# Attention scores of a two-layer trunk in three rounded terms, with the scores of heads 0 to 3 behind the second q projection

## The chip, the cores and the metric

The kernel runs on one core of one Trainium2 chip. The metric is the time of the whole program on the device in microseconds. Before the change three runs gave a median of 249.99 us (249.98 to 250.0).

## What is computed

Two layers of a decoder trunk over 256 positions of width 1024. Each layer normalises x, projects it with one matrix of 3584 columns, and feeds three branches: eight heads of a mixture of dilated causal attention, a linear recurrence of width 256, and four heads of stick-breaking attention. The branches are gated and projected back. For this change these parts of the reference matter:

```
qa = apply_partial_rope(a_q.reshape(b, s, N_HEADS_DIL, HEAD_DIM), cos, sin)   # 8 heads of 64
ka = apply_partial_rope(a_k.reshape(b, s, N_HEADS_DIL, HEAD_DIM), cos, sin)
...
s = jnp.einsum('bhqd,bhqjd->bhqj', q_blk, k_g)            # dilated: the union of three patterns
...
z = jnp.einsum('bhqd,bhkd->bhqk', q_blk, kf) * scale      # stick-breaking, 4 heads, no rope
...
y = jnp.concatenate([y_a, y_b, y_c], axis=-1)
return x + jnp.einsum('bse,ed->bsd', y, w_out)
```

All inputs and outputs are float32. The kernel computes every score of a head as a product of q and k over 64 dimensions: query tile 0 (queries 0 to 127) against 128 keys, query tile 1 against 256 keys, the causal and pattern masks being added afterwards.

## The kernel before

Activations are held transposed, so that a projection of 256 columns gives q or k of four heads as two blocks of 128 partitions, two heads of 64 dimensions in each. The weights come from memory in chunks of 1 MB (`load_chunk`, L101): each is loaded in two halves, and each quarter is rounded on ScalarE (L109, tile `whi`) and its rest formed on VectorE (L110, `wlo` = weight minus `whi`). Activations are split alike (`xh`, `xl`). A projection is the sum of three rounded matmul products, high by high, high by rest and rest by high (`mm3`, L211; in layer 1 `proj_b` joins two of them, L329 and L332, and adds the parts on VectorE, L337). The chunks go through four buffers and are asked for up to two ahead (`ask`, `weights`).

The order on TensorE is the program's order, written by hand; on the other engines a scheduler arranges the instructions of the same program, and each engine then runs its list in order. `proj_b` takes an argument `mid`: work that is put between the two halves (blocks of 128 columns) of a projection. In a layer the projections of this stretch come in this order: q and k of the stick-breaking heads (`qc`, `kc`), q and k of dilated heads 0 to 3 (`CH_AQ[0]`, `CH_AK[0]`), the recurrence's input (`CH_BX`, inside `conv`), q and k of heads 4 to 7 (`CH_AQ[1]`, `CH_AK[1]`), then the gates CG, BG and AG.

Scores are plain float32 matmuls (L443 for the stick-breaking heads in `sb_scores`, L497 for the dilated heads in `dil_scores`). A call makes four heads; the two heads of a pair use different halves of TensorE's rows and stand next to each other in the order. Each head's scores fill one PSUM bank (128 x 384 used) of the pool `at`, which has four banks under the tag "s"; the transposes of weights and probabilities (`turned`, L463) and the gate matmuls use the same four in turn. Projections use three banks of the pool `pp`.

Behind the stick-breaking scores ScalarE makes two sigmoids a head (L449, L450, shown at L83) and VectorE two scans and a product (L454, L456). Behind the dilated scores VectorE subtracts the mask and takes the row minimum (L504), ScalarE exponentiates, and VectorE divides (L515, L517). q and k of the dilated heads are rotated on VectorE (`rotate`, L481 to L484). The convolution is VectorE work as well (L544, L546), and GpSimd sends its result to memory positions in the other half (L549). GpSimd does little else: small constants at the start of the program (L274 to L290), two single-column operations per norm, and clearing one column pair per head (L452).

Of the kernel before, what the change touches and what calls it, by code (L numbers as in the profile page):

```python
# [9 lines left out]
F32 = mybir.dt.float32  # L10
# [5 lines left out]
P = 128  # L16
# [32 lines left out]
def trunk_kernel(ctx: ExitStack, tc: tile.TileContext, x, first_x, first, wpack, prm_d, gatew, gains, consts, rope, out):  # L49
# [247 lines left out]
    for l in range(L):  # L297
# [5 lines left out]
        def y_half(h):  # L303
            ys[h] = [sb.tile([P, 4, S], F32R, name=n, tag=f"{n}{h}") for n in ("yh", "yl")]

        y_half(0)

        def proj_a(ps, w, t, kb, nk, cw, first, last):
            v = [a.rearrange("p (k c) -> p k c", c=cw) for a in w]
            ts_ = slice(t * P, t * P + P)  # L310
# [3 lines left out]
        def proj_b(c, mid=None, to=None, sc=1.0):  # L314
            pair = c in PAIRED[l]
            hi, lo = [a.rearrange("p (k c) -> p k c", c=256) for a in weights(l, c, AHEAD - 1 if mid else AHEAD)]
            if pair:
                flat = None if to is not None else scr(512)
                to = v2(flat) if to is None else to
            else:  # L320
                flat = bank(pp, "pp")
            for b in range(2):
                cs = slice(b * P, b * P + P)
                if pair:
                    ps = bank(pp, "pp")
                    seq = [(0, k) for k in range(NK - 1)] + [(1, k) for k in range(NK)] + [(0, NK - 1)]
                    for i, (is_lo, k) in enumerate(seq):
                        if is_lo:
                            pe.matmul(ps[:, 0:S], lo[:, k, cs], xh[:, k, :], start=False, stop=False,  # L329
                                      skip_group_check=True)  # L330
                        else:
                            pe.matmul(ps, hi[:, k, cs], xx[:, k].rearrange("p h t -> p (h t)"), start=i == 0,  # L332
                                      stop=i == len(seq) - 1, skip_group_check=True)
                    low = wk.tile([P, S], F32, name="low", tag="low", bufs=2)
                    act.activation(low, ps[:, S:2 * S], AF.Copy, scale=sc)  # L335
                    if sc == 1.0:
                        dve.tensor_add(to[:, b, :], ps[:, 0:S], low)  # L337
                    else:
                        dve.scalar_tensor_tensor(to[:, b, :], ps[:, 0:S], sc, low, ALU.mult, ALU.add)
                else:  # L340
                    mm3(flat[:, b * 256:(b + 1) * 256], [lambda k, a=a: a[:, k, cs] for a in (hi, lo)],
                        [lambda k, a=a: a[:, k, :] for a in (xh, xl)], range(NK), True, True)
                if b == 0 and mid:
                    mid()
                    ask(l, c)
            return flat

        def proj_to(dst, c, mid=None, sc=1.0):
            if l > 0 and c in PAIRED[l]:
                proj_b(c, mid, dst, sc)  # L350
            else:
                scaled(dst, proj_b(c, mid), sc)
# [65 lines left out]
        def head(h):  # L418
            return slice((h % 2) * HD, (h % 2) * HD + HD), h // 2, slice(h * HD, (h + 1) * HD)
# [13 lines left out]
        zs, sw = {}, {}  # L433
        halves = ((0, slice(0, 128)), (1, slice(128, 384)))

        def sb_scores():
            for p in (0, 2):
                for h in (p, p + 1):
                    zs[h] = bank(at, "s")
                for t, cs in halves:  # L440
                    for h in (p, p + 1):
                        hr, hb, _ = head(h)
                        pe.matmul(zs[h][:, cs], qc[hr, hb, t * P:(t + 1) * P], kc[hr, hb, 0:(t + 1) * P],  # L443
                                  start=t == 0, stop=True, skip_group_check=True)
            table(SIGM, [split[l, CH_AK[0]]])
            for h in range(NHC):
                z = zs[h][:, 0:384]
                bt, om = scr(384), scr(384)
                tab(om, z, AF.Sigmoid, scale=-1.0)  # L449
                tab(bt, z, AF.Sigmoid)  # L450
                w = sw[h] = wk.tile([P, 384], F32, name="sw", tag="sw", bufs=4)
                gps.memset(w[:, 127::256], 0.0)  # L452
                for lo, n in ((0, 127), (128, 255)):
                    dve.tensor_tensor_scan(w[:, lo:lo + n][:, ::-1], om[:, lo + 1:lo + 1 + n][:, ::-1],  # L454
                                           diag[:, 255 - n:255][:, ::-1], 0.0, ALU.mult, ALU.add)
                dve.tensor_mul(w, bt, w)  # L456
# [19 lines left out]
        def rotate(ps, tiles, h0, tag):  # L476
            dst = tiles[h0] = sb.tile([P, 2, S], F32, name=tag, tag=tag)
            rt_ = rp0 if l == 0 else rp
            cc, ss = [rt_[:, i:i + 1, :].broadcast_to([P, 2, S]) for i in range(2)]
            sw = scr(512)  # L480
            dve.stream_shuffle(sw, ps, SHUF)  # L481
            dve.tensor_mul(dst, v2(ps), cc)
            dve.tensor_mul(v2(sw), v2(sw), ss)
            dve.tensor_add(dst, dst, v2(sw))  # L484
# [3 lines left out]

        def dil_scores(h0):
            sps = {}  # L490
            for p in (h0, h0 + 2):
                for h in (p, p + 1):
                    sps[h] = bank(at, "s")
                for t, cs in halves:
                    for h in (p, p + 1):
                        hr, hb, _ = head(h - h0)
                        pe.matmul(sps[h][:, cs], qT[h0][hr, hb, t * P:(t + 1) * P], kT[h0][hr, hb, 0:(t + 1) * P],  # L497
                                  start=True, stop=True)
            shifted = {}
            for h in range(h0, h0 + 4):  # L500
                xs = scr(384)
                mn = wk.tile([P, 2], F32, name="mn", tag="mn", bufs=4)
                for t, cs in halves:
                    dve.tensor_tensor_reduce(xs[:, cs], sps[h][:, cs], nmask[:, cs], -0.125, 3e38,  # L504
                                             ALU.add, ALU.min, mn[:, t:t + 1])
                shifted[h] = xs, mn
            return shifted
# [26 lines left out]
        it = sb.tile([P, 2, S], F32, name="it", tag="it")  # L534
        th = sb.tile([P, 2, S], F32, name="th", tag="th")
        bg = sb.tile([P, 2, S], F32, name="bg", tag="bg")
        ag = sb.tile([P, 4, S], F32, name="ag", tag="ag")
        cg = sb.tile([P, 2, S], F32, name="cg", tag="cg")

        def conv(mid):  # L540
            dve.memset(bxp[:, :, 0:3], 0.0)
            proj_to(bxp[:, :, 3:259], CH_BX, mid)
            for b in range(2):
                dve.tensor_scalar(xc[:, b, :], bxp[:, b, 3:259], prm[:, b, 3:4], prm[:, b, 4:5], ALU.mult, ALU.add)  # L544
                for j in (2, 1, 0):
                    dve.scalar_tensor_tensor(xc[:, b, :], bxp[:, b, j:j + 256], prm[:, b, j:j + 1], xc[:, b, :],  # L546
                                             ALU.mult, ALU.add)
            for j in range(2):
                gps.dma_start(out=xs[j * HD:(j + 1) * HD], in_=xc[(1 - j) * HD:(2 - j) * HD])  # L549
# [38 lines left out]
        if l == 0:  # L588
            ck_ps = proj_b(CH_CK, rows_of_rstd)
            scaled(qc, cq_ps, 0.125)  # L590
            scaled(kc, ck_ps)
        else:
            proj_to(kc, CH_CK)
        if l == 0:
            for i in range(2):
                dve.tensor_mul(rp0[:, i, :], rp[:, i, :], rb)
        rotate(proj_b(CH_AQ[0], sb_scores), qT, 0, "q0")
        rotate(proj_b(CH_AK[0]), kT, 0, "k0")
        sw_t, sw_heads = turned_tile()
        conv(lambda: turned(sw, 0, (0,), sw_t))  # L600
        turned(sw, 0, (1, 2), sw_t)
        y_c = {}

        def second():
            table(LN_EXP)
            dil_softmax(dil_scores(0))

        rotate(proj_b(CH_AQ[1], second), qT, 4, "q1")
        rotate(proj_b(CH_AK[1]), kT, 4, "k1")
        table(SIGM)  # L610
        cg_ps = proj_b(CH_CG)
        pts = dil_transposes(0)
        silu(cg, cg_ps)


        def third():
            lru_gates()
# [7 lines left out]
        lru_scan()  # L625
        emit_y(rt, bg, 0, 2)
        dil_softmax(y_c["s"])
        ps = proj_b(CH_AG)
        table(SIGM)
        silu(ag[:, 0:2, :], ps)  # L630
# [145 lines left out]
```

## Time and profile before

| what | value |
|---|---|
| median of three runs | 249.99 us |
| the profiled execution: device time | 248.82 us |
| the profiled execution: span | 246.7 us |
| granted TensorE clock, mean | 0.996 |
| TensorE matmuls busy | 239.0 us (97% of the span) |
| VectorE busy | 196.5 us (80%) |
| ScalarE busy | 167.2 us (68%) |
| GpSimd busy | 12.1 us (5%) |

The profile is one execution. Its device time is 1.2 us below the median of the runs, and 2.1 us above its own span. In its rows PE is TensorE, DVE VectorE, ACT ScalarE, POOL GpSimd and SP the queue that issues most transfers. A row of the chain that ended last has start, length and what ran; a row of a timeline has start, length, engine, line, operation, tiles, shape and count, and in brackets the idle time before it with what ended it. A float32 matmul stands in the rows as two instructions, so a call of eight score matmuls is x16.

### The profile page before, as it was taken

Reading aid. Unit: us, or ns where it says so; the run is one execution under the profiler, and the core shown is the slowest. Engines: PE = TensorE matmul, PEld = TensorE weight load, DVE = VectorE, ACT = ScalarE, POOL = GpSimd, SP = SyncE. Lnnn points to the kernel's source line nnn. Section 1 sums busy time; section 2 is a strip of 40 time slices with the busy share of each in tenths; the row PEclk is TensorE's granted clock in tenths of the full one; section 3 lists DMA queues with packets and bytes.
Section 4 is the critical chain, followed back from the end, with each engine's and each line's share of the span. In section 5 each row is a group of like instructions: output and inputs, shape, how many; then the busy total and the mean of one; then the engine's idle time right before and its main releaser. Section 6 shows DMA issues by size and latency. Waiting matters only on the chain.

```text
span 246.7 us, 4531 instructions
## 1 busy us (share of the span) xinstructions
PE 239.0 (97%) x1657; PEld 212.1 (86%) x1657; DVE 196.5 (80%) x442; ACT 167.2 (68%) x360; POOL 12.1 (5%) x45
## 2 busy tenths in 40 slices
PE   8999999999999999999999999999999999999990
PEld 4889999999998899878889988889889889987870
DVE  3885699999999799985792766999999987985253
ACT  3778989735947499964662885865498649992142
POOL 0037000001000000000100000000010000000000
PEclk9999999999999999999999999999999999999998
DMA  6989889268447741277157486605553672000022
GB/s 201 404 292 403 342 288 333 96 215 268 134 157 255 258 117 56 85 240 284 74 189 232 142 268 243 200 7 165 161 157 119 197 262 98 0 0 3 0 85 85
DMA packets 13173, 43.89 MB, mean 178 GB/s; under 512 B 1632, under 2 KB 2144, under 8 KB 13152
## 3 DMA queue, kind: packets, MB, share of 16 engines
q1 hardware_dynamic: 12384, 42.30, 51.1%
q10 hardware_dynamic: 576, 0.79, 0.9%
q0 software_dynamic: 192, 0.52, 0.7%
q8 instruction: 13, 0.21, 0.4%
q14 instruction: 8, 0.07, 0.1%
HBM read 42.03 MB, written 1.05 MB: 175 GB/s over the span
## 4 chain that ended last, share of the span: by engine, by line
PE 94%; DMA 2%; DVE 1%; ACT 1%; SPq 0%; issue 0%; ACTq 0%
PE pp L211 51%; PE pp L332 11%; PE s L211 9%; PE pp L329 5%; PE s L169 4%; PE s L463 3%; PE s L497 2%; PE y L427 2%; DMA st<-first 2%; PE pp L169 2%; PE s L443 1%; PE pp L427 1%; PE s L557 1%; PE s L259 1%; DVE xres L668 0%; ACT scr L242 0%
## 5 line engine op out<-in xcount | busy, mean ns | idle before, releaser
L110 DVE TENSOR_TENSOR wlo<-st,whi 128x512 fp32r<-128x512 f32 x132 | 84.1, 683 | 12.8 <-ACT whi L109 12.5
L109 ACT ACTIVATE whi<-st 128x512 fp32r<-128x512 f32 x132 | 73.9, 629 | 28.0 <-PE pp L211 11.8
L211 PE MATMUL pp<-xx,whi 128*128 128x256 f32 x480 | 63.3, 285 | 0.0
L211 PEld LDWEIGHTS pp<-xx,whi 128*128 128x128 f32 x480 | 59.7, 191 | 1.4 <-issue 1.3
L211 PE MATMUL pp<-xx,wlo 128*128 128x256 f32 x240 | 33.7, 283 | 0.0
L211 PEld LDWEIGHTS pp<-xx,wlo 128*128 128x128 f32 x240 | 30.9, 192 | 0.0
L332 PE MATMUL pp<-xx,whi 128*128 128x512 f32 x112 | 29.3, 396 | 0.0
L332 PEld LDWEIGHTS pp<-xx,whi 128*128 128x128 f32 x112 | 20.1, 189 | 4.1 <-ACT scr L83 0.3
L77 ACT ACT_TABLE_LOAD x13 | 16.7, 1283 | 1.9 <-PEq L769 1.7
L83 ACT ACTIVATE pr<-scr,mn 128x128 f32<-128x128 f32 (+1 forms) x32 | 14.1, 442 | 5.2 <-DVE mn L504 5.2
L329 PEld LDWEIGHTS pp<-xx,wlo 128*128 128x128 f32 x112 | 15.3, 190 | 1.1
L329 PE MATMUL pp<-xx,wlo 128*128 128x256 f32 x112 | 15.6, 282 | 0.0
L211 PE MATMUL pp<-whi,yh 128*128 128x512 f32 x48 | 14.5, 403 | 0.0
L211 PE MATMUL pp<-wlo,yh 128*128 128x512 f32 x48 | 14.0, 393 | 0.0
L211 PE MATMUL pp<-whi,yl 128*128 128x512 f32 x48 | 14.0, 393 | 0.0
L335 ACT ACTIVATE low<-pp 128x256 f32<-128x256 f32 x14 | 5.3, 382 | 9.1 <-PE pp L332 6.8
L211 PEld LDWEIGHTS pp<-wlo,yh 128*128 128x128 f32 x48 | 9.0, 188 | 2.1
L211 PEld LDWEIGHTS pp<-whi,yl 128*128 128x128 f32 x48 | 9.0, 188 | 2.0
L211 PEld LDWEIGHTS pp<-whi,yh 128*128 128x128 f32 x48 | 8.6, 188 | 2.0 <-issue 0.3
L169 PE MATMUL s<-whi,xx 128*128 128x512 f32 (+1 forms) x36 | 10.2, 404 | 0.1
L415 ACT ACTIVATE yh<-scr 128x512 fp32r<-128x512 f32 x8 | 5.0, 631 | 7.7 <-DVE scr L413 7.6
L504 DVE CUSTOM_DVE_ANT_0 scr<-s,con 128x128 f32<-128x128 f32 (+1 forms) x32 | 9.2, 351 | 0.0
(165 smaller groups left out, 355.2 us busy)
## 6 DMA issues: line engine op xcount, KB each, us to landing
st<-w_pack SPq DMA_DIRECT2D x66, 512.0 KB, 5.4
st<-first SPq DMA_DIRECT2D x7, 512.0 KB, 6.2
xres<-x_in SPq DMA_DIRECT2D x2, 512.0 KB, 8.1
gw_t<-gate_w SPq DMA_DIRECT2D x2, 256.0 KB, 6.9
gn<-gains SPq DMA_DIRECT2D x1, 512.0 KB, 6.7
xs<-xc POOLq DMA_DIRECT2D x4, 128.0 KB, 3.7
gf<-gains SPq DMA_DIRECT2D x1, 512.0 KB, 6.8
out<-scr SPq DMA_DIRECT2D x2, 256.0 KB, 2.1
```

The source lines that it names most:

```text
L77: load = act.preload_act_table_set(name)
L83: i = dep(act.activation(*a, **k), loaded["load"])
L109: split[l, c] = act.activation(hi[:, ws], st[:, ss], AF.Copy)
L110: dve.tensor_sub(lo[:, ws], st[:, ss], hi[:, ws].bitcast(F32))
L169: pe.matmul(ps[t][:, c0 - base:c1 - base], a[:, k, t * P:(t + 1) * P], b[:, c0:c1], start=k == 0 and i == 0 and c0 == base, stop=k == NK - ...
L211: pe.matmul(ps, a(k), b(k), start=first and i == 0, stop=last and i == len(seq) - 1)
L329: pe.matmul(ps[:, 0:S], lo[:, k, cs], xh[:, k, :], start=False, stop=False, skip_group_check=True)
L332: pe.matmul(ps, hi[:, k, cs], xx[:, k].rearrange("p h t -> p (h t)"), start=i == 0, stop=i == len(seq) - 1, skip_group_check=True)
L335: act.activation(low, ps[:, S:2 * S], AF.Copy, scale=sc)
L427: pe.matmul(y[hr, p * 128 + o:p * 128 + 256], vt[:, s0, hs], wts[i][s0], start=s0 == 0, stop=s0 == 1)
L463: pe.transpose(tp[:, i * P:(i + 1) * P], tiles[h0 + h][:, j * P:(j + 1) * P], ident)
L504: dve.tensor_tensor_reduce(xs[:, cs], sps[h][:, cs], nmask[:, cs], -0.125, 3e38, ALU.add, ALU.min, mn[:, t:t + 1])
```

## The change

The plain float32 score matmuls go. A new function `split_keys` rounds q and k of four heads (GpSimd casts q; k is copied by ScalarE for the stick-breaking heads and heads 0 to 3, and cast by GpSimd for heads 4 to 7), and GpSimd forms both rests. `scores` then sums three rounded products per head and query tile: q by k, rest of q by k, q by rest of k. The results are the same scores in the same PSUM banks.

The order changes in four places of each layer. The stick-breaking scores move from the middle of the first q projection into the middle of the first k projection. The scores of heads 0 to 3 and their softmax move from the middle of the second q projection behind it. The transposes of the stick-breaking weights, which stood in the middle of the recurrence's projection and behind it, now stand together behind the second k projection. Without work in the middle, a projection asks for its second chunk ahead at its start. To hold the split tiles, the buffers `yh0`, `yl0`, `ag`, `q0` and `k0` are used before their old owners need them; these are now created later.

```
+        def split_keys(h0, q, k, tags):
+            parts = []
+            for full, tag in ((q, tags[1:]), (k, tags[0])):
+                if full is q and len(tag) == 2:
+                    hi, lo = [sb.tile([P, 2, S], F32R, name="qk3", tag=t) for t in tag]
+                else:
+                    both = sb.tile([P, 2, 2, S], F32R, name="qk3", tag=tag if full is k else tag[0])
+                    hi, lo = both[:, 0], both[:, 1]
+                if full is k and h0 != 4:
+                    act.activation(hi, full, AF.Copy)
+                else:
+                    gps.tensor_copy(hi, full)
+                gps.tensor_sub(lo, full, hi.bitcast(F32))
+                parts.append((hi, lo))
+            (qh, ql), (kh, kl) = parts
+            exact[h0] = (qh, kh), (ql, kh), (qh, kl)
+
+        def scores(ps, h0, p):
+            for t, cs in halves:
+                for n, (a, b) in enumerate(exact[h0]):
+                    for h in (p, p + 1):
+                        hr, hb, _ = head(h)
+                        pe.matmul(ps[h][:, cs], a[hr, hb, t * P:(t + 1) * P], b[hr, hb, 0:(t + 1) * P],
+                                  start=n == 0, stop=n == 2, skip_group_check=True)
...
-                for t, cs in halves:
-                    for h in (p, p + 1):
-                        hr, hb, _ = head(h)
-                        pe.matmul(zs[h][:, cs], qc[hr, hb, t * P:(t + 1) * P], kc[hr, hb, 0:(t + 1) * P],
-                                  start=t == 0, stop=True, skip_group_check=True)
+                scores(zs, "sb", p)
...
+        split_keys("sb", qc, kc, ("yh0", "yl0"))
...
-        rotate(proj_b(CH_AQ[0], sb_scores), qT, 0, "q0")
-        rotate(proj_b(CH_AK[0]), kT, 0, "k0")
-        sw_t, sw_heads = turned_tile()
-        conv(lambda: turned(sw, 0, (0,), sw_t))
-        turned(sw, 0, (1, 2), sw_t)
+        rotate(proj_b(CH_AQ[0]), qT, 0, "q0")
+        rotate(proj_b(CH_AK[0], sb_scores), kT, 0, "k0")
+        split_keys(0, qT[0], kT[0], ("yh0", "yl0"))
+        conv(None)
...
-        rotate(proj_b(CH_AQ[1], second), qT, 4, "q1")
+        q1_ps = proj_b(CH_AQ[1])
+        second()
+        rotate(q1_ps, qT, 4, "q1")
+        sw_t, sw_heads = turned_tile()
         rotate(proj_b(CH_AK[1]), kT, 4, "k1")
+        turned(sw, 0, range(3), sw_t)
+        split_keys(4, qT[4], kT[4], ("ag", "q0", "k0"))
         table(SIGM)
         cg_ps = proj_b(CH_CG)
```

What this does to the lists of the engines shows at three places of layer 0. On TensorE, around the scores of heads 0 to 3, before (each pair of L211 rows is one half of a projection; q_640 and k_709 are q and k of heads 0 to 3, sw the stick-breaking weights):

```order
L463 MATMUL s<-con,sw 128x128 x8
L211 MATMUL pp<-xx,whi 128x256 x16
L211 MATMUL pp<-xx,wlo 128x256 x8
L497 MATMUL s<-k_709,q_640 128x128 x2
L497 MATMUL s<-k_709,q_640 128x256 x2
L497 MATMUL s<-k_709,q_640 128x128 x2
L497 MATMUL s<-k_709,q_640 128x256 x2
L211 MATMUL pp<-xx,whi 128x256 x16
L211 MATMUL pp<-xx,wlo 128x256 x8
```

and now (qk_734 is the split q, qk_737 the split k; the line numbers are those of the changed kernel):

```order
L211 MATMUL pp<-xx,whi 128x256 x16
L211 MATMUL pp<-xx,wlo 128x256 x8
L458 MATMUL s<-qk_737,qk_734 128x128 x6
L458 MATMUL s<-qk_737,qk_734 128x256 x6
L458 MATMUL s<-qk_737,qk_734 128x128 x6
L458 MATMUL s<-qk_737,qk_734 128x256 x6
L211 MATMUL pp<-xx,whi 128x256 x16
L211 MATMUL pp<-xx,wlo 128x256 x8
L211 MATMUL pp<-xx,whi 128x256 x16
L211 MATMUL pp<-xx,wlo 128x256 x8
L484 MATMUL s<-con,sw 128x128 x12
```

The scores stand behind both halves of the second q projection instead of between them, and the twelve transposes of the stick-breaking weights, of which eight stood two rows ahead, follow both halves of the second k projection.

On VectorE, from the end of the rotation of k of heads 0 to 3 to the first reduction of their scores, before (L484 ends the rotation, L392 empties the recurrence's projection, L544 and L546 are the convolution, L504 the reduction):

```order
L484 TENSOR_TENSOR k_709<-k_709,scr 128x512
L110 TENSOR_TENSOR wlo<-st,whi 128x512 x6
L392 SCALAR_TENSOR_TENSOR bxp<-pp,rb 128x2x256
L110 TENSOR_TENSOR wlo<-st,whi 128x512
L544 TENSOR_SCALAR xc<-bxp,prm_t 128x256 x2
L546 SCALAR_TENSOR_TENSOR xc<-bxp,prm_t,xc 128x256 x6
L504 ISA scr,mn<-s,con 128x128
```

and now:

```order
L505 TENSOR_TENSOR k_728<-k_728,scr 128x512
L110 TENSOR_TENSOR wlo<-st,whi 128x512 x3
L390 SCALAR_TENSOR_TENSOR bxp<-pp,rb 128x2x256
L110 TENSOR_TENSOR wlo<-st,whi 128x512
L560 TENSOR_SCALAR xc<-bxp,prm_t 128x256 x2
L562 SCALAR_TENSOR_TENSOR xc<-bxp,prm_t,xc 128x256 x6
L110 TENSOR_TENSOR wlo<-st,whi 128x512 x6
L521 ISA scr,mn<-s,con 128x128
```

Six rests of weights stand between the convolution and the reductions, where there were none; three fewer stand ahead of it.

On GpSimd, between the last of the small constants and its transfers of the convolution's result in layer 0 (qk_523 and qk_526 are the split q and k of the stick-breaking heads), the difference is:

```order
 L290 TENSOR_SCALAR nc_290<-c_289 128x4
-L452 MEMSET sw 128x2 x4
-L549 DMA xs<-xc 64x512 x2
+L447 CAST qk_523<-qc 128x512
+L448 TENSOR_TENSOR qk_523<-qc,qk_523 128x512
+L448 TENSOR_TENSOR qk_526<-kc,qk_526 128x512
+L447 CAST qk_734<-q_594 128x512
+L448 TENSOR_TENSOR qk_734<-q_594,qk_734 128x512
+L448 TENSOR_TENSOR qk_737<-k_728,qk_737 128x512
+L565 DMA xs<-xc 64x512 x2
```

Six operations of 128x512 now stand ahead of the transfers, the last of them waiting for the copy of k on ScalarE.

More of the change, by code (lines that the diff above doesn't have):

```diff
@@ L304, in y_half @@
             ys[h] = [sb.tile([P, 4, S], F32R, name=n, tag=f"{n}{h}") for n in ("yh", "yl")]
-        y_half(0)
         def proj_a(ps, w, t, kb, nk, cw, first, last):
@@ L434, in trunk_kernel @@
         halves = ((0, slice(0, 128)), (1, slice(128, 384)))
+        exact = {}
+        def split_keys(h0, q, k, tags):
[21 more added lines that the diff above has]
+                                  start=n == 0, stop=n == 2, skip_group_check=True)
         def sb_scores():
@@ L490, in dil_scores @@
             sps = {}
-            for p in (h0, h0 + 2):
+            for p in (0, 2):
                 for h in (p, p + 1):
                     sps[h] = bank(at, "s")
[L494 to L498, printed above, removed]
+                scores(sps, h0, p)
             shifted = {}
@@ L503, in dil_scores @@
                 for t, cs in halves:
-                    dve.tensor_tensor_reduce(xs[:, cs], sps[h][:, cs], nmask[:, cs], -0.125, 3e38,
+                    dve.tensor_tensor_reduce(xs[:, cs], sps[h - h0][:, cs], nmask[:, cs], -0.125, 3e38,
                                              ALU.add, ALU.min, mn[:, t:t + 1])
@@ L536, in trunk_kernel @@
         bg = sb.tile([P, 2, S], F32, name="bg", tag="bg")
-        ag = sb.tile([P, 4, S], F32, name="ag", tag="ag")
         cg = sb.tile([P, 2, S], F32, name="cg", tag="cg")
@@ L613, in trunk_kernel @@
         silu(cg, cg_ps)
+        y_half(0)
         def third():
@@ L627, in trunk_kernel @@
         dil_softmax(y_c["s"])
+        ag = sb.tile([P, 4, S], F32, name="ag", tag="ag")
         ps = proj_b(CH_AG)
```

## The prediction

> **What bounds the kernel now.** I read the page first, then the chain that ended last in order of time, then the timelines of VectorE (DVE), TensorE (PE) and GpSimd (POOL) around the scores, and the busy time of three stretches.
>
> ```profile
> PE 239.0 (97%) x1657; PEld 212.1 (86%) x1657; DVE 196.5 (80%) x442; ACT 167.2 (68%) x360; POOL 12.1 (5%) x45
> ...
> PE 94%; DMA 2%; DVE 1%; ACT 1%; SPq 0%; issue 0%; ACTq 0%
> ...
> L109 ACT ACTIVATE whi<-st 128x512 fp32r<-128x512 f32 x132 | 73.9, 629 | 28.0 <-PE pp L211 11.8
> ```
>
> ```profile
> 31.68 5.75 PE pp L211 x48
> 37.43 1.51 PE s L443 x16
> 38.94 11.71 PE pp L211 x96
> ...
> 57.72 1.51 PE s L497 x16
> 59.23 14.59 PE pp L211 x120
> ...
> 81.78 1.51 PE s L497 x16
> ...
> 155.44 1.51 PE s L443 x16
> ...
> 175.25 1.51 PE s L497 x16
> ...
> 185.34 5.76 PE pp L211 x48
> ```
>
> PE carries the chain without a gap: from 31.68 to 185.34 the next row always starts where the last one ended. So every microsecond by which the scores shrink comes off, and every wait put in front of PE is added. A set of scores (four heads) is 1.51 us, a projection half (24 matmuls) is 5.75 / 2 = 2.87. But VectorE has hardly any room where the change works:
>
> ```profile
> core 0: us, PE busy (x) PEld busy (x) DVE busy (x) ACT busy (x) POOL busy (x), PEclk, DMA share, GB/s
> 34.50:68.00 33.50, 33.50 (x286) 32.48 (x285) 33.06 (x86) 24.53 (x55) 1.66 (x6) 1.00 0.67 219
> 68.00:100.00 32.00, 32.00 (x279) 29.84 (x278) 29.68 (x71) 23.76 (x54) 0.00 (x0) 1.00 0.51 161
> 141.50:185.50 44.00, 44.00 (x271) 38.01 (x270) 38.44 (x97) 30.91 (x71) 1.09 (x2) 1.00 0.54 175
> ```
>
> In layer 0 VectorE is busy 33.06 of the 33.5 us from 34.5 to 68.0, the stretch in which the change moves its work. The clock is 1.00, so it plays no part.
>
> **1. The six score sets themselves.** The two heads of a pair stand on different halves of the rows and run together. These rows are single moments inside one set; their first column is the start of the oldest matmul still running.
>
> ```profile
> 37.69 0.59 PE L443 MATMUL s<-kc,qc 64*128 64x256 f32 x3
> 37.91 0.60 PE L443 MATMUL s<-kc,qc 64*128 64x256 f32 x5
> 38.12 0.60 PE L443 MATMUL s<-kc,qc 64*128 64x128 f32 x5
> 38.23 0.49 PE L443 MATMUL s<-kc,qc 64*128 64x128 f32 x3
> ```
>
> A pair of 256 columns advances by 37.91 - 37.69 = 0.22, one of 128 by 38.23 - 38.12 = 0.11. The code has 8 matmuls per set and the chain x16, so each plain fp32 matmul is two instructions: 4 pair slots of 0.11 and 4 of 0.22 make 1.3, and 0.2 goes to entering and leaving. The change has 24 instructions, 12 slots: 6 of 256 columns, 6 of 128. Rounded matmuls of 256 columns take 2.87 / 24 = 0.12, so the long slots are 0.72. Rounded matmuls of 128 columns are nowhere in the trace: from below, half of 0.12, 0.06; from above, the fp32 instruction's 0.11. I take 0.087, the middle, as neither row is nearer. Sum 0.72 + 0.52 + 0.2 = 1.45, by the ends 1.28 to 1.58, against 1.51: -0.06 a set (-0.2 to +0.1). The three terms save almost nothing.
>
> **2. VectorE's order in layer 0.** Its rows give the prices of the sum:
>
> ```profile
> 36.47 1.93 DVE L110 TENSOR_TENSOR wlo<-st,whi 128x512 fp32r<-128x512 f32 x3
> 38.84 1.31 DVE L454 TENSOR_TENSOR_SCAN sw<-scr,con 128x127 f32<-128x127 f32 x3 [0.44 <-ACT scr L83]
> ...
> 44.91 0.74 DVE L481 STREAM_SHUFFLE scr<-pp 128x512 f32<-128x512 f32 x1
> ...
> 49.75 0.74 DVE L481 STREAM_SHUFFLE scr<-pp 128x512 f32<-128x512 f32 x1
> ...
> 52.78 3.70 DVE L110 TENSOR_TENSOR wlo<-st,whi 128x512 fp32r<-128x512 f32 x6
> 56.39 0.69 DVE L392 SCALAR_TENSOR_TENSOR bxp<-pp,rb 128x512 f32<-128x512 f32 x1
> ...
> 57.59 0.73 DVE L544 TENSOR_SCALAR xc<-bxp,prm_t 128x256 f32<-128x256 f32 x2
> ...
> 60.62 0.28 DVE L504 CUSTOM_DVE_ANT_0 scr<-s,con 128x128 f32<-128x128 f32 x1
> ...
> 61.17 0.28 DVE L504 CUSTOM_DVE_ANT_0 scr<-s,con 128x128 f32<-128x128 f32 x1
> ```
>
> A weight rest (L110) is (56.39 - 52.78) / 6 = 0.60; a rotation with the rest inside it 52.78 - 49.75 = 3.0; the convolution 60.62 - 57.59 = 3.0; the evacuation of bxp and the rest behind it 1.2 together; one head's two reductions 0.55; the stick-breaking scans of four heads with one rest 6.1, so about 6.7 with two.
>
> VectorE after, from 36.47: five rests, 39.5; then it waits for the end of the first q projection, which is no longer cut by scores: 34.56 + 2 x 2.87 = 40.3, with the semaphore 40.55. Rotation of q 43.6, four rests 46.0, scans 6.7 to 52.7, rotation of k 55.7, three rests, bxp, a rest (3.0) 58.7, convolution 61.8, six rests 65.4, reductions of two heads, a rest, the third head: 67.65. Before, the reductions began at 60.6; now seven more rests (4.2) stand ahead of them. PE after: 40.3, half of k 2.87, a set 1.5, the other half, BX and the second q projection 5 x 2.9, a set 1.5, the second k projection 5.8, two groups of transposes 0.88: 67.4. The third group takes the PSUM bank of the third head, free at 67.65. So by order alone VectorE is 0.3 late here, and faster sets ahead of this point would only wait longer. In layer 1 the same sum gives 0.1 (the second half of the second q projection takes the PSUM bank of the first BX half, which VectorE empties behind the k rotation) and 0.25 at the third group; its breaks between matmul kinds are one fewer, 0.15 back.
>
> **3. The splits on POOL.** The change gives POOL ten operations of 128x512 a layer (three for the stick-breaking heads, three for heads 0 to 3, four for heads 4 to 7). Before has none of that size, but its small ones show what happens beside a busy VectorE:
>
> ```profile
> 18.34 0.22 POOL L285 TENSOR_SCALAR ls<-ls 128x4 f32<-128x4 f32 x1
> 18.64 0.57 POOL L284 TENSOR_TENSOR ls<-ls,ls 128x4 f32<-128x4 f32 x1
> 19.30 0.54 POOL L285 TENSOR_SCALAR ls<-ls 128x4 f32<-128x4 f32 x1
> 19.92 0.20 POOL L284 TENSOR_TENSOR ls<-ls,ls 128x4 f32<-128x4 f32 x1
> 20.20 0.22 POOL L285 TENSOR_SCALAR ls<-ls 128x4 f32<-128x4 f32 x1
> ```
>
> ```profile
> 18.46 1.29 DVE L110 TENSOR_TENSOR wlo<-st,whi 128x512 fp32r<-128x512 f32 x2 [1.05 <-ACT whi L109]
> 20.61 1.29 DVE L110 TENSOR_TENSOR wlo<-st,whi 128x512 fp32r<-128x512 f32 x2 [0.85 <-ACT whi L109]
> ```
>
> ```profile
> 122.63 0.87 POOL L195 TENSOR_SCALAR ss<-sq 128x1 f32<-128x1 f32 x1 [5.91 <-ACT scr L193]
> ```
>
> With VectorE idle (19.92, 20.20) such an operation takes 0.20 to 0.22. While the two rests of 18.46 to 19.75 run it takes 0.54 to 0.57, and at 122.63 even 0.87: POOL gets through only when a VectorE operation ends. They take turns. What no row shows is the reverse, a POOL operation long enough to hold VectorE up; I take it that turns go both ways, for VectorE operations that read two SBUF tensors (rests, scans, the convolution's steps, the end of a rotation). The Trainium skill says this outright (SBUF — State Buffer, section "SBUF: two separate sides"): the two engines share a port pair as an exclusive lock held for a whole instruction, and the other one blocks; the POOL rows agree with it for POOL.
>
> ```profile
> 153.10 0.42 DVE L337 TENSOR_TENSOR kc<-pp,low 128x256 f32<-128x256 f32 x1 [2.24 <-ACT low L335]
> ```
>
> A POOL operation's size: 0.2 fixed (the 128x4 rows) plus VectorE's streaming of 512 columns, twice the difference of the row of 512 at 56.39 and this one of 256: 2 x (0.69 - 0.42) = 0.54. That is 0.75 for a cast; for a subtraction, which reads two tensors, 0.75 if it streams as VectorE does, 1.28 if the inputs take turns. I take 1.0, the middle, since no row is nearer to either. The Trainium skill (GPSIMD Engine Reference, section 3.1) has 4497 ns for an add of 2048 columns, an estimate of 1.1 for 512; the sum by that would be near mine.
>
> Layer 0 with turns: the stick-breaking split holds VectorE for 0.75, 0.4 (the rest lies beside kc's evacuation, which reads one SBUF tensor) and 1.0, less 1.0 of the idle time ahead of 40.55: +1.2. The q split of heads 0 to 3 adds 1.75, the k rest 1.0. Third head reduced at 67.65 + 4.0 = 71.7, with the semaphores 71.85; the last transposes end at 72.3. Before, PE was at the same work at 59.23 + 3 x 2.92 = 67.98: **+4.3 us**. Part of it shows earlier: PE waits about 1.4 at the scores, since k is rotated at 55.7 + 2.95 = 58.7, copied on ACT 0.63 later (L109's mean, the same operation), and its rest, behind the VectorE operation that is running, comes at about 60.9, against 59.5 when PE wants the third term. In layer 1 the stick-breaking split falls into VectorE's gaps, such as the 2.24 ahead of kc at 153.10, so 2.75 are left, of which 0.4 lie beside one-input work: with the 0.2 of order **+2.5 us**. The third split's four operations (3.5 us a layer) have 81.78 - 67.98 = 13.8 us between the second k projection and their scores, and VectorE's 2.3 us of idle time between 68 and 100; I cost them at nothing, and at up to 1.2 a layer if that cover is short.
>
> **Edits at nothing.** The stick-breaking transposes are the same 12, behind the second k projection. ACT's two copies a layer (0.63 each) meet an idle share of a quarter; the k copy waits at the head of ACT's queue for the rotation, with weight roundings and, in layer 1, the second BX evacuation behind it, whose bank PE takes for the second k projection, some 2 us later by the same sum. POOL's DMA of xc waits behind the k rest; the gates that read it stand behind the CG projection. SP asks for chunks a little earlier, at a DMA share of 0.67.
>
> **Sum.** 4.3 + 2.5 + 2 x (-0.06) for the sets of heads 4 to 7 (the other four sets lie ahead of a wait) = +6.7. The profiled execution is 248.82, so 255.5; the median of the runs, 249.99, stands 1.2 above it, so **256.7**. With subtractions of 0.75 and short slots +4.9, 254.9; with 1.28 and part of the third split's 1.2 +9.5, 259.5.
>
> **Rivals.** *VectorE doesn't wait for POOL*: only the late order stays, 0.3 + 0.2 - 0.1, 250.4 (249.4 to 251.0). For it: the rests of 18.46 and 20.61 are as long as any. Chance 0.18.
> *Faster*: pair slots of 128 columns at 0.06, and a VectorE that waits for nothing on POOL and empties the third head's bank 0.5 earlier than I sum. From the point where that bank is free before PE arrives, all six sets count: 1.28 against 1.51, 6 x -0.23 = -1.4, 248.6. Against it: VectorE's 33.06 of 33.5. The Trainium skill (FP8 and Floating Point Precision, "TensorE Precision Notes") gives true fp32 four passes, so three terms are three quarters: 1.3 x 3/4 + 0.2, 1.18 a set, -2.0 in all, 248.0. The trace has 2 x 0.22 against 0.12, 3.7 passes, which nearly agrees. Chance 0.13.
> *The rounded terms don't run as said*: 128 columns cost two fp32 instructions, 0.22, as the same product did before. Then 0.72 + 1.32 + 0.2 = 2.24 a set, +0.73 x 6, with POOL at no cost: 254.4. For it: no rounded matmul under 256 columns in the trace. Chance 0.10.
>
> **Chances.** The forecast has 0.59. A measurement of this kernel tells 0.2% (0.5 us) from no change. Faster: the second rival and 0.02 of the first, 0.15. Same: 0.10, from the first. Slower: 0.75. The range runs from 249.8 to 259.5; what is left out is the faster rival, the low end of the first and 0.04 above.
>
> **What would show it.** In the new profile: PE waits at the scores of heads 0 to 3 for POOL's last rest, and at the moved transposes for VectorE's reductions; POOL rows of 0.75 to 1.3 us, longer beside VectorE; rests of VectorE well over 0.68 us; sets of 1.3 to 1.6 us without their waits; layer 0 loses more than layer 1. VectorE operations that stay at 0.68 beside POOL's, or a PE without waits, would prove the forecast wrong; sets over 2 us would point to the third rival.

## The result, and the profile after

Four runs gave a median of 258.34 us (258.05 to 258.58) against 249.99 us (249.46 to 250.0) for the kernel before: a ratio of 1.0339, 95% interval 1.0321 to 1.0357. The prediction said 256.7 us, 249.8 to 259.5, slower. Of the profiled executions, the one after took 258.26 us and the one before 248.82.

First the page of the profile after: busy times, the chain that ended last by engine, and VectorE's weight rests (busy, mean ns).

```profile
PE 242.8 (95%) x1705; PEld 214.7 (84%) x1705; DVE 210.1 (82%) x442; ACT 169.1 (66%) x364; POOL 37.9 (15%) x65
...
PE 58%; DVE 26%; DMA 6%; issue 5%; ACT 3%; SPq 1%; DVEq 0%; ACTq 0%
...
L110 DVE TENSOR_TENSOR wlo<-st,whi 128x512 fp32r<-128x512 f32 x132 | 94.4, 761 | 12.7 <-ACT whi L109 12.6
```

The chain was TensorE at 94%; now VectorE holds 26% of it. VectorE has the same 442 instructions and is busy 13.6 us longer; the 132 rests take 761 ns in the mean where they took 683. TensorE is busy only 3.8 us longer in a span that grew by 9.8, so it waits. What TensorE waited for in the profile after, from the view of waits (total, times, longest):

```profile
PE s L484 <- DVE mn L521: 2.6, 3, 1.6
...
PE s L458 <- POOL qk L448: 1.1, 1, 1.1
PE pp L330 <- DVE scr L335: 0.8, 1, 0.8
...
PE pp L330 <- DVE bxp L335: 0.4, 1, 0.4
```

Where these waits lie, from TensorE's timeline of layer 0 (L458 are the scores of heads 0 to 3, L484 the moved transposes):

```profile
61.59 1.42 PE L458 MATMUL s<-qk,qk 64*128 64x128 f32 x20 [1.08 <-POOL qk L448]
...
70.53 1.21 PE L484 MATMUL s<-con,sw 128*128 128x128 f32 x8 [1.58 <-DVE mn L521]
72.24 1.12 PE L484 MATMUL s<-con,sw 128*128 128x128 f32 x4 [0.50 <-DVE mn L521]
```

Both waits stand where the prediction put them: at the scores for GpSimd's last rest, at the transposes for VectorE's reductions. GpSimd's timeline of the same stretch, with its six operations (the casts L447, the subtractions L448):

```profile
34.93 1.60 POOL L447 CAST qk<-qc 128x512 fp32r<-128x512 f32 x1 [9.18 <-DVE qc L390]
36.62 1.87 POOL L448 TENSOR_TENSOR qk<-qc,qk 128x512 fp32r<-128x512 f32 x1
38.45 1.74 POOL L448 TENSOR_TENSOR qk<-kc,qk 128x512 fp32r<-128x512 f32 x1
45.75 0.92 POOL L447 CAST qk<-q 128x512 fp32r<-128x512 f32 x1 [5.56 <-DVE q L505]
46.75 1.62 POOL L448 TENSOR_TENSOR qk<-q,qk 128x512 fp32r<-128x512 f32 x1
60.01 1.53 POOL L448 TENSOR_TENSOR qk<-k,qk 128x512 fp32r<-128x512 f32 x1 [11.64 <-ACT qk L445]
```

And VectorE's timeline, of which these are the groups of rests that stand beside them, and a later one that stands alone:

```profile
37.30 5.25 DVE L110 TENSOR_TENSOR wlo<-st,whi 128x512 fp32r<-128x512 f32 x5
...
45.52 4.00 DVE L110 TENSOR_TENSOR wlo<-st,whi 128x512 fp32r<-128x512 f32 x4
...
59.13 2.96 DVE L110 TENSOR_TENSOR wlo<-st,whi 128x512 fp32r<-128x512 f32 x3
...
66.23 3.69 DVE L110 TENSOR_TENSOR wlo<-st,whi 128x512 fp32r<-128x512 f32 x6
```

Six rests without a GpSimd operation beside them (66.23) take 3.69, as before. So five would take 3.1, four 2.5 and three 1.9; they take 5.25, 4.00 and 2.96. VectorE loses 2.2 + 1.5 + 1.1 = 4.8 us ahead of its reductions. Some 0.9 of this would have been idle time otherwise, an estimate: five rests from 37.30 would end at 40.4, and the first q projection, by the prediction's 40.55 and 0.7 of start-up, at 41.3. A little later GpSimd begins the third split. Its timeline:

```profile
77.68 0.61 POOL L447 CAST qk<-q 128x512 fp32r<-128x512 f32 x1 [6.44 <-DVE q L505]
...
78.38 1.29 POOL L448 TENSOR_TENSOR qk<-q,qk 128x512 fp32r<-128x512 f32 x1
```

VectorE's timeline of the same moments, inside the rotation of the second k:

```profile
78.12 0.67 DVE L503 TENSOR_TENSOR k<-pp,rp 128x512 f32<-128x512 f32 x1
78.71 1.51 DVE L504 TENSOR_TENSOR scr<-scr,rp 128x512 f32<-128x512 f32 x1
```

This shows which operations collide. L503 reads one of its tensors from PSUM and keeps its 0.67 beside the subtraction of 78.38; L504 reads two from SBUF, usually 0.68, and ends after the subtraction does. The cast of 77.68 and the subtraction of 78.38 give GpSimd's own times: 0.61 and 1.29.

In layer 1 it isn't only operations with two tensors that collide. From the timelines of GpSimd and VectorE there:

```profile
182.50 1.30 POOL L448 TENSOR_TENSOR qk<-k,qk 128x512 fp32r<-128x512 f32 x1 [10.49 <-ACT qk L445]
```

```profile
182.55 1.40 DVE L560 TENSOR_SCALAR xc<-bxp,prm_t 128x256 f32<-128x256 f32 x1
```

L560, the first step of the convolution, reads one tensor from SBUF and two values a row; before it took 0.41. With two rests at 169.16 that take 1.70 instead of 1.28 and three scans at 170.78 that take 2.40 instead of 1.31, VectorE loses 0.4 + 1.1 + 1.0 = 2.5 us in this part of layer 1.

Then the chain from the transposes on, in layer 0 and at the same points of layer 1:

```profile
73.36 6.83 PE pp L211 x48
...
88.15 1.58 PE s L458 x24
...
148.05 1.61 PE pp L330 x7
...
194.84 5.75 PE pp L211 x48
...
208.55 1.58 PE s L458 x24
```

And busy times by stretch, with the granted clock (PEclk) behind the wait:

```profile
core 0: us, PE busy (x) PEld busy (x) DVE busy (x) ACT busy (x) POOL busy (x), PEclk, DMA share, GB/s
...
72.00:74.00 2.00, 1.76 (x8) 1.76 (x9) 1.95 (x14) 1.98 (x10) 0.00 (x0) 0.57 1.04 401
74.00:76.00 2.00, 2.00 (x12) 2.00 (x12) 2.00 (x9) 1.99 (x3) 0.00 (x0) 0.58 0.66 264
76.00:78.00 2.00, 2.00 (x19) 2.00 (x19) 1.97 (x5) 2.00 (x5) 0.32 (x1) 1.00 0.00 0
```

The transposes of layer 0 end at 73.36 where before had 67.98: 5.4 later, of which 0.7 is a later start-up of this execution (the matmuls ahead of its first q projection), so 4.6 to 4.7. The CG projection behind them takes 6.83, not 5.75, at a clock of 0.57: another 1.1. Layer 1 begins at 148.05 (141.47 before, +6.6), and its CG projection at 194.84 (185.34, +9.5): layer 1 adds 2.9. A set of scores that waits for nothing is 1.58, not 1.51.

### The profile page after: what moved, and what is told of

Same layout as the page of the kernel before. It is cut to its first block, busy times and chain, and to the rows that moved or that the text cites. A ratio compares the mean times of both kernels' runs of the same rounds, so it can differ in the third digit from the quotient of the medians.

```text
span 256.5 us, 4661 instructions
## 1 busy us (share of the span) xinstructions
PE 242.8 (95%) x1705; PEld 214.7 (84%) x1705; DVE 210.1 (82%) x442; ACT 169.1 (66%) x364; POOL 37.9 (15%) x65
## 4 chain that ended last, share of the span: by engine, by line
PE 58%; DVE 26%; DMA 6%; issue 5%; ACT 3%; SPq 1%; DVEq 0%; ACTq 0%
PE pp L211 34%; DVE wlo L110 11%; PE s L211 9%; PE pp L330 4%; DVE sw L475 3%; DMA xres<-x_in 3%; PE s L484 3%; DMA st<-first 3%; PE y L425 2%; PE pp L327 2%; DVE xc L562 2%; DVE sw L477 2%; DVE scr L521 1%; PE s L458 1%; DVE scr L502 1%
## 5 line engine op out<-in xcount | busy, mean ns | idle before, releaser
L110 DVE TENSOR_TENSOR wlo<-st,whi 128x512 fp32r<-128x512 f32 x132 | 94.4, 761 | 12.7 <-ACT whi L109 12.6
L211 PE MATMUL pp<-xx,whi 128*128 128x256 f32 x480 | 64.4, 288 | 0.0
L211 PEld LDWEIGHTS pp<-xx,whi 128*128 128x128 f32 x480 | 60.8, 195 | 0.5
L211 PE MATMUL pp<-xx,wlo 128*128 128x256 f32 x240 | 33.7, 283 | 0.0
L211 PEld LDWEIGHTS pp<-xx,wlo 128*128 128x128 f32 x240 | 31.0, 192 | 0.0
L330 PEld LDWEIGHTS pp<-xx,whi 128*128 128x128 f32 x112 | 20.1, 189 | 5.6 <-DVE scr L335 1.2
L211 PE MATMUL pp<-whi,yh 128*128 128x512 f32 x48 | 14.5, 405 | 0.0
L211 PE MATMUL pp<-whi,yl 128*128 128x512 f32 x48 | 14.1, 396 | 0.0
L211 PE MATMUL pp<-wlo,yh 128*128 128x512 f32 x48 | 14.1, 395 | 0.0
L458 PE MATMUL s<-qk,qk 64*128 64x128 f32 (+1 forms) x144 | 10.1, 283 | 1.1 <-POOL qk L448 1.1
L211 PEld LDWEIGHTS pp<-whi,yl 128*128 128x128 f32 x48 | 9.0, 188 | 2.2
L211 PEld LDWEIGHTS pp<-wlo,yh 128*128 128x128 f32 x48 | 9.0, 188 | 2.2
L458 PEld LDWEIGHTS s<-qk,qk 64*128 64x128 f32 x144 | 8.7, 186 | 2.4 <-POOL qk L448 1.2
L169 PE MATMUL s<-whi,xx 128*128 128x512 f32 (+1 forms) x36 | 9.6, 379 | 1.1 <-ACT xx L153 0.6
L211 PEld LDWEIGHTS pp<-whi,yh 128*128 128x128 f32 x48 | 8.7, 188 | 2.0 <-issue 0.3
```

What stands on the lines that cost most here:

```text
L110: dve.tensor_sub(lo[:, ws], st[:, ss], hi[:, ws].bitcast(F32))
L169: pe.matmul(ps[t][:, c0 - base:c1 - base], a[:, k, t * P:(t + 1) * P], b[:, c0:c1], start=k == 0 and i == 0 and c0 == base, stop=k == NK - ...
L211: pe.matmul(ps, a(k), b(k), start=first and i == 0, stop=last and i == len(seq) - 1)
L458: pe.matmul(ps[h][:, cs], a[hr, hb, t * P:(t + 1) * P], b[hr, hb, 0:(t + 1) * P], start=n == 0, stop=n == 2, skip_group_check=True)
```

## The experiments

Theory: GpSimd's splits hold up VectorE's operations on SBUF, and VectorE's late reductions hold up TensorE. Rivals: the order alone; the three terms themselves; another collision than that of the two engines.

**The order without the splits.** The changed order, with plain float32 scores and no splits:

```
-                for n, (a, b) in enumerate(exact[h0]):
...
+                for h in (p, p + 1):
+                    hr, hb, _ = head(h)
+                    pe.matmul(ps[h][:, cs], q[hr, hb, t * P:(t + 1) * P], k[hr, hb, 0:(t + 1) * P],
+                              start=True, stop=True, skip_group_check=True)
...
-        split_keys("sb", qc, kc, ("yh0", "yl0"))
```

> The changed order of the work, but plain float32 scores and no splits. Theory (VectorE and GpSimd take turns, and that makes the time): without GpSimd's ten operations a layer only the later reductions on VectorE are left, so 250.4 us (249.8 to 251.0), VectorE's weight rests at 0.68 us again. Rival (the order itself makes the time): 254 us or more, with the same waits of TensorE ahead of the moved transposes as in the changed kernel, 2 us in layer 0.

Measured: 252.11 us, 1.0085 (1.005 to 1.012), above the range, and with a wide spread (249.92 to 254.87): its profiled run is the fastest. There TensorE waits neither at the scores nor at the moved transposes. But the scheduler gave VectorE another list: four rests ahead of the reductions, not six. So this doesn't price the changed list; it says that the order, as arranged here, costs 2.1 us by the ratio and not 8. Where the 2.1 come from in the longer runs stays open, as the profiled one doesn't show them.

**The splits without their use.** All splits stay where they are; the scores are plain float32 products that don't read them (the edit above, with the calls of `split_keys` kept).

> The changed order with all of the splits on GpSimd and ScalarE, but the scores are plain float32 matmuls that don't read the splits. Theory (turns): 257 to 258.5 us, since VectorE loses the same time to GpSimd; TensorE no longer waits at the scores and waits the longer at the moved transposes. Rival (the three terms make the time, by their 24 matmuls a set and by the wait for the last rest): 250 to 251 us.

Measured: 261.11 us, 1.0443 (1.0412 to 1.0473). The three terms aren't the cause: without them the kernel is slower still. Its waits of TensorE:

```profile
PE s L458 <- ACT rt L83: 2.5, 1, 2.5
PE s L573 <- ACT pa L485: 2.3, 1, 2.3
```

The size was 2.6 us above what was expected. VectorE's list changed here too (four rests ahead), and the lateness comes out at ScalarE instead. The first wait is at the scores of heads 4 to 7: beside the third split VectorE's six rests ahead of the CG gate take 5.18 us (3.69 without a neighbour), ScalarE's gates come late, and the clock behind the wait is granted at 0.55 and 0.59 for 4 us. The second is in layer 1. So the third split isn't free when TensorE comes early. Whether that is all that it costs more than the change itself wasn't tested.

**The splits without GpSimd.** The same three terms; ScalarE makes all roundings, VectorE all rests.

```
-                if full is k and h0 != 4:
-                    act.activation(hi, full, AF.Copy)
-                else:
-                    gps.tensor_copy(hi, full)
-                gps.tensor_sub(lo, full, hi.bitcast(F32))
+                act.activation(hi, full, AF.Copy)
+                dve.tensor_sub(lo, full, hi.bitcast(F32))
```

> The changed kernel with every cast of the splits on ScalarE and every rest on VectorE, nothing on GpSimd: VectorE gets six more operations of 0.6 us a layer, two of which lie in idle time. Theory (turns): VectorE's own rests cost less than GpSimd's, about 1.5 us in layer 0 and 1.2 in layer 1, and the sets 0.07 each at heads 4 to 7: 253 us (252 to 254.5). Rival (the order or the three terms make the time): 257 to 260 us, since nothing of that changed and VectorE has more to do.

Measured: 256.63 us, 1.0262 (1.0228 to 1.0295), above the range of the theory and just below that of the rival, so the time alone decides for neither. The group of rests on VectorE in its profile:

```profile
L110 DVE TENSOR_TENSOR wlo<-st,whi 128x512 fp32r<-128x512 f32 x132 | 84.3, 684 | 11.5 <-ACT whi L109 11.3
```

And what TensorE waited for:

```profile
PE s L570 <- ACT pa L482: 1.2, 2, 0.8
...
PE s L455 <- ACT it L83: 0.4, 1, 0.4
PE s L211 <- ACT yh L413: 0.4, 1, 0.4
```

The rests are back at 684 ns, so the lengthening came with GpSimd. For the reductions TensorE now waits 0.4 us at the moved transposes (2.6 in the change). But the work now lies on VectorE and ScalarE, and TensorE waits mostly for ScalarE. By the ratios, taking GpSimd out wins back 0.77 of the 3.39%.

**The wait filled.** In layer 0 nine unused matmuls keep TensorE at work while it waits for the reductions; they come between the second k projection and the transposes and before the third group.

```
+            fill(7)
+            turned(sw, 0, (0, 1), sw_t)
+            fill(2)
+            turned(sw, 0, (2,), sw_t)
```

> The changed kernel, in layer 0 with seven float32 matmuls of 128x128 whose result nobody reads ahead of the moved transposes and two ahead of their third group, where TensorE stands idle. Theory (the 1.1 us that the CG projection behind them takes more is the clock, granted at 0.57 for 4 us after that idle time): the projection takes 5.75 us again and the whole 257.3 us. Rival (the slower projection waits for its operands or is disturbed otherwise): no difference, 258.3 us, or slower by the added matmuls.

Measured: 257.92 us, 1.0321 (1.0301 to 1.0342) against 1.0339 for the change: not told apart. In its profile, on TensorE's timeline, the third group, the transposes of the probabilities behind the CG projection, and the scores of heads 4 to 7:

```profile
72.45 0.66 PE L484 MATMUL s<-con,sw 128*128 128x128 f32 x4
...
78.70 1.48 PE L484 MATMUL s<-con,pr 128*128 128x128 f32 x12
...
88.28 0.95 PE L458 MATMUL s<-qk,qk 64*128 64x128 f32 x11 [0.40 <-ACT it L83]
```

The third group stands 0.2 later than in the change, yet the probabilities' transposes come at 78.70 (80.03 there, by its chain 80.19 for the end of the projection): the projection runs at full clock again (granted at 1.00 in every stretch of 2 us from 66 to 80). That part came as the theory said, the whole time did not: of the gain of 1.3 about 0.8 is given back at the next scores, which wait for ScalarE's gates, so the projection behind them starts at 89.17 against 89.66.

**The collision by itself.** These four take the kernel before and put GpSimd operations into layer 0, behind the first q rotation, that nobody reads. The lists of TensorE, VectorE and ScalarE in their traces are those of before, operation by operation.

```
-        rotate(proj_b(CH_AQ[0], sb_scores), qT, 0, "q0")
+        rotate(proj_b(CH_AQ[0], sb_scores), qT, 0, "q0"); [gps.tensor_sub(ys[0][1][:, 0:2], qT[0], qc) for _ in range(10 if l == 0 else 0)]
```

The others have five subtractions, ten fillings (`gps.memset` of the same tile, behind one small subtraction that sets their start) and ten casts (`gps.tensor_copy`).

> The kernel before, with ten unused 128x512 subtractions on GpSimd in layer 0, started by the rotation of the first q (about 48 us) and read by nobody; the order of every other engine is that of before. Theory (VectorE and GpSimd take turns on operations that read two SBUF tensors): in the changed kernel VectorE lost 2.2 + 1.5 + 1.1 = 4.8 us beside splits that take 2 x 0.61 + 4 x 1.29 = 6.4 us alone, three quarters; ten subtractions are 12.9, so VectorE loses 7 to 11 us between 48 and 70. Its first reduction, at 60.6 before, comes at 67.5 to 72, its weight rests there last 1.0 us or more in the mean, and TensorE begins to wait behind 73 us, where before has some 7 us of room: kernel 252 to 256. Rival (only GpSimd waits): VectorE's first reduction stays at 60.6 within 0.5, kernel 249.8 to 250.3.

> As with the ten subtractions, but five. Theory: VectorE loses half, 3.5 to 5.5 us, first reduction at 64 to 66.5; TensorE's room of some 7 us behind covers it, kernel 249.8 to 251.5. Rival: first reduction at 60.6, kernel 249.8 to 250.3.

> The kernel before, with ten fillings (memset) of 128x512 on GpSimd at the same place in place of the ten subtractions: GpSimd writes the same bytes and reads nothing. If what holds VectorE is GpSimd's use of SBUF as such, VectorE loses about as much as GpSimd's fillings last (first reduction at 64 to 68, kernel 250 to 253). If it is GpSimd's reading of two inputs, first reduction at 60.6 within 0.5 and kernel 249.8 to 250.3.

> The kernel before, with ten casts of 128x512 on GpSimd (one SBUF tensor read) at the same place in place of the ten subtractions. A cast takes 0.61 us alone, ten 6.1, about as much as five subtractions (6.4), which cost VectorE 4.4 us and the kernel 5.3. If every GpSimd operation that reads SBUF holds VectorE, the first reduction comes at 64 to 67 and the kernel at 252.5 to 256. If it is the second input that does it, the first reduction stays at 60.6 to 62 (start-up included) and the kernel at 249.8 to 250.3, as with the fillings.

| added on GpSimd | VectorE's first reduction, later by | us, ratio to before (95%) |
|---|---|---|
| ten subtractions | 9.9 | 260.66, 1.0443 (1.0420 to 1.0466) |
| five subtractions | 4.4 | 255.36, 1.0211 (1.0169 to 1.0252) |
| ten casts | 3.3 | 253.70, 1.0163 (1.0128 to 1.0198) |
| ten fillings | 0.0 | 250.07, 1.0016 (1.0000 to 1.0032) |

The second column is counted from the start of the first q rotation in each trace (before: 60.62 - 44.91 = 15.71), so that start-up drops out. With ten subtractions, GpSimd's timeline:

```profile
48.77 17.09 POOL L597 TENSOR_TENSOR yl<-q,qc 128x512 fp32r<-128x512 f32 x10 [22.75 <-DVE q L484]
```

and VectorE's six rests ahead of bxp, which before took 3.70:

```profile
57.85 9.17 DVE L110 TENSOR_TENSOR wlo<-st,whi 128x512 fp32r<-128x512 f32 x6
```

With ten fillings, which end among the same six rests, GpSimd's timeline:

```profile
50.40 5.20 POOL L597 MEMSET yl<- 128x512 f32 x9
```

and VectorE's:

```profile
54.45 3.69 DVE L110 TENSOR_TENSOR wlo<-st,whi 128x512 fp32r<-128x512 f32 x6
```

With ten casts, GpSimd's timeline:

```profile
48.99 9.97 POOL L597 CAST yl<-q 128x512 fp32r<-128x512 f32 x10 [22.93 <-DVE q L484]
```

and VectorE's:

```profile
55.36 5.34 DVE L110 TENSOR_TENSOR wlo<-st,whi 128x512 fp32r<-128x512 f32 x6
```

The loss follows the dose, 0.9 to 1.0 us of VectorE for each subtraction and 0.33 for each cast. Fillings write the same bytes and read nothing, and VectorE doesn't notice them; nor does the kernel, by more than 0.3%. So GpSimd's reading of SBUF is what holds these rests up, and a single tensor read is enough. Whether fillings would hold an operation like L560 isn't shown.

Start-up aside, VectorE's first reduction came about where one of the readings expected it in all four, but the kernel's time missed upward with both doses of subtractions: 260.66 where 252 to 256 was expected, and 255.36 where TensorE's 7 us of room should have covered the 4.4 (249.8 to 251.5). The chain of the run with five shows the reason:

```profile
74.91 1.81 DVE wlo L110 x3
...
76.74 4.57 DMA st<-w_pack
...
81.33 0.63 ACT whi L109
81.96 0.49 ACT pa L464
...
82.50 1.08 PE s L557 x12
```

Late rests free the staging buffers of the weights late; the next chunk lands at 81.31; ScalarE stands at that chunk's rounding with the evacuation of the transposes (`pa`) queued behind; and TensorE waits 2.7 us for that evacuation (4.0 with ten subtractions). The room was that of VectorE's results, not that of the transfers it releases.

**A part of the change that should be free.** The kernel before, with heads 4 to 7 alone in three terms, and there only the tile of 256 columns; four splits on GpSimd a layer.

```
+                    terms = exact[h0] if t and h0 in exact else [(qT[h0], kT[h0])]
+                    for n, (a, b) in enumerate(terms):
```

> The kernel before, with heads 4 to 7 alone in three terms, and of these only the tile of 256 columns (the one of 128 stays a plain fp32 product); their four splits on GpSimd behind the second k rotation, as in the change. By the slots a set is 4 x 0.11 + 6 x 0.12 + 0.2 = 1.36 against 1.51, 0.15 off in each layer, if the splits stay covered as they were in the changed kernel: 249.5 (ratio 0.999). Rival: the turns of GpSimd and VectorE delay VectorE by some 3 us at 74 us, where it feeds the gates and the next reductions: 250.5 to 253. The gain looked for is at the edge of what can be measured.

Measured: 250.73 us, 1.0055 (1.0034 to 1.0077). The set itself, on the chain in layer 1, is as long as the slots say:

```profile
201.46 1.35 PE s L512 x20
```

1.35 against 1.51 before, and still the kernel loses about 1.4 us by the ratio (1.0 by the medians): the splits cost more than the sets give. The loss is in layer 0, where beside the splits three rests take 3.40 us and four 3.99 (1.88 and 2.48 before); in layer 1 the kernel keeps pace (it is 2.4 us behind at the start of that layer, 1.1 of it start-up, and 2.4 at its last scores). No variant here beats the kernel before.

## Why the prediction was right, and where its sizes were off

1. *What bounds the kernel.* Right: VectorE had no room in layer 0, and it moved onto the chain (26%).
2. *The sets.* I took 0.087 for a rounded slot of 128 columns, between 0.06 and 0.11. (1.58 - 0.2 - 6 x 0.12) / 6 = 0.11, the upper end: +0.07 a set, not -0.06. The set of 1.35 agrees: 4 x 0.11 + 6 x 0.12 + 0.2 = 1.36. So in 128 columns three terms cost half as much again as float32, not less.
3. *The order.* The 0.3 that it costs alone wasn't tested with the changed list; with a milder list the order cost 2.1 by the ratio. The trace of the change bears the 0.3 out as an estimate: the third head is reduced at 72.2; less 0.7 of start-up and the 4.8 - 0.9 = 3.9 that VectorE lost to GpSimd, that is 67.6, and the sum had 67.65. The 2.1 of the other list are above what the rival that VectorE doesn't wait had asked for (250.4), so its price was probably too low.
4. *The splits.* The mechanism is shown, by the trace and by the dose. Two sizes were off and largely cancelled: the subtraction is 1.29 alone, at my upper bound of 1.28 and not the 1.0 I took (the cast 0.61, not 0.75), but I counted all of a GpSimd operation as lost to VectorE, and the dose shows 0.99 of 1.29 for a subtraction and 0.33 of 0.61 for a cast. That they cancelled is luck. So VectorE lost 4.8 in layer 0 (3.9 without the idle time), where the sum had 4.9 (3.9 without its 1.0); TensorE's wait at the scores was 1.08 against 1.4; layer 0 came out at 4.6 against 4.3, layer 1 at 2.9 against 2.5. The condition was too narrow: I named the convolution's steps among the operations that read two SBUF tensors, but the first of them, L560, reads one and waited as well. The Trainium skill (SBUF — State Buffer, "SBUF: two separate sides") adds a limit that I hadn't used: VectorE's two-input operations contend only with a GpSimd operation that reads SBUF. Fillings at 0.0 us and casts at 3.3 agree with that.
5. *The third split at nothing.* Right for the changed kernel as far as TensorE's waits show: the scores of heads 4 to 7 wait for nothing at 88.15 and 208.55. In the kernel before, where nothing else makes TensorE late, four splits a layer for heads 4 to 7 made the whole 1.4 us slower although the sets were shorter, and with the splits unused TensorE waited 2.5 us at these scores. The cover was that TensorE was already late.
6. *The clock.* The prediction held that it plays no part. It fell to 0.57 behind the new wait, 1.1 us there. The filled wait shows that the gap causes it, and that removing it hardly moves the end.
7. *The rivals.* That VectorE doesn't wait for GpSimd falls with the rests of 5.25, 4.00 and 2.96 and with the dose. The faster one falls with the slot of 0.11. That rounded terms of 128 columns cost two float32 instructions falls with sets of 1.58 where it asked for 2.24.

The forecast was 1.6 us short. The sum of the trace is 4.6 + 1.1 + 2.9 + 0.1 for the two free sets, 8.7, and 8.35 by the medians; the predicted sum was 6.7. The terms that were off are the clock (1.1, put at nothing), the two layers (0.3 and 0.4) and the two free sets (0.14 + 0.12 = 0.26). The range was ten microseconds wide, so that the time fell into it says little; the waits at the two places and the lengthened rests say more.

## What to carry to other kernels

Idle time of GpSimd is not free where VectorE is full: each of its operations that reads SBUF stops those of VectorE that work on SBUF alone, here for half to three quarters of its own length, while fillings cost VectorE's weight rests nothing. Count the slots of TensorE by width before trading one float32 product for three rounded ones: at 256 columns three terms were cheaper (0.36 against 0.44), at 128 dearer (0.33 against 0.22). When room is claimed for a late engine, follow also what its late work releases, the next transfer above all.

## What the runs showed of the hardware

TensorE's clock fell after short gaps. In the change, idle times of 1.58 and 0.50 us around 1.2 us of transposes (68.9 to 72.2) were followed by 0.57 and 0.58 until 76. With five subtractions, the stretches behind the wait of 2.7 us, which ended at 82.5, were (columns as above, the clock third from the end):

```profile
82.00:84.00 2.00, 1.50 (x16) 0.84 (x18) 2.00 (x5) 2.00 (x5) 0.00 (x0) 0.92 0.81 256
84.00:86.00 2.00, 2.00 (x18) 1.45 (x16) 2.00 (x4) 2.00 (x6) 0.00 (x0) 0.50 0.84 285
86.00:88.00 2.00, 2.00 (x20) 1.32 (x17) 1.56 (x3) 1.11 (x3) 0.00 (x0) 0.72 0.80 262
```

The clock goes to one half (0.50) for about 2 x (0.08 + 0.50 + 0.28) / 0.5 = 3.4 us, as in the change: 2 x (0.43 + 0.42) / 0.5 = 3.4. It falls after the gap, when TensorE is at work again, so the price of a wait is paid a second time. The same sum gives 3.4 us again with ten casts, behind a wait of 2.2 us (2 x (0.02 + 0.50 + 0.33) / 0.5 from 80 to 86), and with ten subtractions, behind idle times of 0.55 and 0.88 us within 2.6 us (2 x (0.46 + 0.39) / 0.5 from 78 to 82). In the change the single gap of 1.08 us at the scores, and that of 0.8 in layer 1, had no such effect. The Trainium skill (TensorE: Matmul & The Clock Gate, Part 1) has the clock at half rate after at least one idle window of about 3.4 us, and at the full rate after a busy one of about that length. The second agrees with the 3.4 us at half rate; the first doesn't, as idle times of 1.4 us within 2.6 us were enough here.
